# A junk row laid elsewhere, and half of the weight low parts on another engine, at the two ends of the first attention

## The chip, the cores and the metric

One core of one Trainium2 chip runs the whole program in one launch. The metric is device time in microseconds (us), given as the median of repeated runs. Five engines work side by side, each through its own list of instructions in order: TensorE (PE in the profile), VectorE (DVE), ScalarE (ACT), GpSimd (POOL) and SyncE (SP), which here only issues DMA transfers. An instruction may wait for others by semaphores. What stands behind a waiting instruction in an engine's list waits too.

## The reference

A two-layer backbone over 1024 latent tokens (`SEQ`) with 256 context tokens (`CTX_LEN`) as a prefix, 1024 wide, all in float32. The first ("even") layer's mixer is what the change touches:

```python
# even_mixer: 8 query heads and 2 key heads of 64, beside a gated linear recurrence of 4 heads of 128
oa_lat, oa_ctx = gqa_axial_attention(...)    # latent queries: softmax over all 1280 keys;
                                             # context queries: over the 256 context keys only
ob_lat, ob_ctx = hgrn2_bidirectional(...)
y_lat = concat([oa_lat, rms_norm(ob_lat) * silu(g)]) @ w_out
y_ctx = concat([oa_ctx, ...]) @ w_out
# the layer around it, for the latent tokens and with gates of their own for the context
x = x + g1 * rms_norm(y_lat, norm_post_mix)
h = rms_norm(x, norm_pre_ffn) * (1.0 + sc2) + sh2
u = conv(h @ w_up); x = x + g2 * rms_norm((silu(u_g) * u_a) @ w_down, norm_post_ffn)
```

The second ("odd") layer has a neighbourhood attention in place of this mixer, and another FFN.

## The kernel before

**Precision.** TensorE multiplies float32 values as fp32r. For more precision the kernel splits a value x into a high part `hi` (ScalarE copies x into an fp32r tile) and a low part `lo` = x - `hi` (a subtraction), and sums three products: hi hi, hi lo, lo hi. The low part of a weight of `w_out` is thus ready only after ScalarE's copy of the same weight.

**The attention.** `even_attention` goes through 40 pairs of a query block (256 queries; the context block first, then four latent blocks) and a head (8), two steps for each pair, each for 128 queries. So the first 16 steps belong to the context block, whose rows have 256 keys; the others have 1280. A step s issues, in this order: `scores` (TensorE into `g_ps` or `a_s`, and a VectorE operation that moves them to `a_p` and finds the row's minimum of the negated scores, L1103), `exponential` of the step before (ScalarE), for even s from 2 to 16 `prepare_w(s/2 - 1)`, some loads, `values` of three pairs earlier, `transposes` of two pairs earlier (TensorE into `a_pt`, L1136; ScalarE's high part `a_ph`, L1137; VectorE's low part `a_pl`, L1138) with one or two pieces of the output projection between them, `divide` of the step before (VectorE's reciprocal `rl`, L1115; GpSimd's multiplication, L1116, the "division" below) and `finish`, which on every second pair sums into `a_oT` (L1172).

**The weights of the output projection.** `prepare_w(m)`, L1056 to 1064, for m from 0 to 7: `w_out` is taken in eight tiles of 128x1024. ScalarE makes `w_hi` from `w_raw` (L1061), GpSimd subtracts into `w_lo` (L1062), and then the load of tile m + 2 is issued into the buffer of tile m, of which there are two (`w_raw`, L1056). The eight tiles fall into the context steps.

**The projection and the norms.** `project` yields one group of three matmuls at a time into `g_ps` (L136 is the line of the helper that issues each matmul), which `step` calls up. Its trailing work, the list `late`, normalizes each row block of 128 tokens: `y_half` squares a projected half on ScalarE, with the squares themselves written to a junk tile named `yjunk` and only their sum kept; VectorE scales by the gate (L364) and adds the old stream `y_x` (loaded at L1216); GpSimd stores it; `squares` squares the new stream on ScalarE, again into a junk tile (`sq_junk`, L1191); `rstd` raises to the power -1/2 on GpSimd (L144); ScalarE scales by it (L1229), and GpSimd stores the normalized rows to `xnd` in DRAM (L1230).

**The FFN behind it.** `ffn_up` begins with loads of `xnd` into tiles `n_x` (L1611), one of 128 tokens each, in the order 8, 9 (the context), 0, 1, 2, 3, then two loads of `w_up` into `w_raw` (L1530), then `n_x` 4 to 7. TensorE transposes them (`n_pv`, `n_pt`, L1344), ScalarE scales and shifts into `n_t` (L1345). The weights are split in pieces, the first of them `w_A11h` (L1546), and the first product goes into `u_g`.

**What sets the order.** The instructions of the attention on all four compute engines and on SyncE are tied to the order in which the code issues them, and so are SyncE's loads at the start of the FFN. The waits of an instruction are set by what it reads and by who last used the memory that it writes. Memory is given out by pools. Tiles of one pool (the attention's is `sp`, named "at") are laid out one behind the other in the order of their first allocation; when a stage ends, its pools' memory goes to the tiles of the next stage. So the tile that the FFN lays over a tile of the attention waits for the last user of that tile. Near the end of the attention's set-up three small tiles are allocated: `zeros` (one column of it is used, the rest is padding in multiples of `LINE`, 32 floats), `pv_t` and `sq_junk`. `sq_junk` lies under the first `n_x` tile of the FFN.

Of the kernel before, what the change touches and what calls it, by code (L numbers as in the profile page):

```python
# [11 lines left out]
F32 = mybir.dt.float32  # L12
F32R = mybir.dt.float32r
BF16 = mybir.dt.bfloat16
AF = mybir.ActivationFunctionType
OP = mybir.AluOpType
# [4 lines left out]
P = 128  # L21
# [18 lines left out]
LINE = 32  # L40
# [25 lines left out]
class Trunk:  # L66
# [958 lines left out]
    def even_attention(self, gp, tp, pp, sp):  # L1025
# [5 lines left out]
        nc, a = self.nc, self.a  # L1031
# [20 lines left out]
        def load_w(m):  # L1052
            if m < 8:
                raws[m] = self.wp.tile([P, 1024], F32, name="w_raw", bufs=2)
                k = 2 * (m % 4)
                nc.sync.dma_start(raws[m].rearrange("p (a b) -> p a b", a=2), w_out[:, k:k + 2, 512 * (m // 4):512 * (m // 4) + 512])  # L1056

        def prepare_w(m):
            raw = raws.pop(m)
            hi, lo = (self.wp.tile([P, 1024], F32R, name="w_" + x, bufs=8) for x in ("hi", "lo"))  # L1060
            nc.scalar.copy(hi, raw)  # L1061
            nc.gpsimd.tensor_tensor(out=lo, in0=raw, in1=hi.bitcast(F32), op=OP.subtract)  # L1062
            W[m] = hi, lo
            load_w(m + 2)

# [121 lines left out]
                st["ready"] = b  # L1187

        def squares(y, ms):
            for h in range(2):  # L1190
                nc.scalar.activation(yjunk, y[:, 512 * h:512 * h + 512], AF.Square, scale=1.0 / 32.0, accum_out=ms[:, h:h + 1])  # L1191

        late = []

# [49 lines left out]
                elif late:  # L1244
                    late.pop(0)()

        zeros = sp.tile([P, 2 * LINE], F32, name="zeros", bufs=1)[:, 0:1]
        nc.vector.memset(zeros, 0.0)
        pv_t = sp.tile([P, QB], F32, name="pv_t", bufs=1)
        yjunk = sp.tile([P, 512], BF16, name="sq_junk", bufs=1)  # L1250
        N = 2 * len(pairs)
        later = {4: lambda: load_keys(0, 0), 6: lambda: load_keys(0, 1), 8: lambda: load_values(0, NT - 2),
                 10: lambda: load_keys(1, 0), 12: lambda: load_keys(1, 1), 14: lambda: load_gate(1)}
# [1 line left out]
        with self.in_order(*self.compute, E.SP):  # L1255
# [8 lines left out]
            for s in range(N + 8):  # L1264
                pair, half = s // 2, s % 2
                if s < N:
                    if half == 0 and pair:
                        load_q(pair + 2)
                    scores(s)
                if 0 <= s - 1 < N:  # L1270
                    exponential(s - 1)
                if 2 <= s < 18 and half == 0:
                    prepare_w(s // 2 - 1)
                later.pop(s, lambda: None)()
                if 0 <= pair - 3 < len(pairs):
                    values(pair - 3, half)
                t = transposes(pair - 2, half) if 0 <= pair - 2 < len(pairs) else iter(())
                next(t, None)
                step(1)
                next(t, None)  # L1280
                step(1)
                next(t, None)
                if 0 <= s - 1 < N:
                    divide(s - 1)
                if 0 <= pair - 3 < len(pairs) and half == 1:
                    finish(pair - 3)
                for _ in range(min(len(todo), 1 + len(todo) // 3)):
                    todo.pop(0)()
# [1579 lines left out]
```

## Time and profile before

| | us |
|---|---|
| median of 3 runs (lowest, highest) | 3322.68 (3320.38, 3323.68) |
| the profiled execution | 3321.63 |
| its span in the trace | 3319.9 |
| mean granted TensorE clock | 0.972 |

The profile is of one execution, whose own time is 1.05 us below the median. The span is what the trace covers; 1.73 us lie around it. The page's first part gives each engine's busy time, its share of the span and its number of instructions. A group's row gives the line, the engine, the operation, output<-input with shapes, the count (x8), then the busy sum in us and the mean of one in ns, and the idle time just before them with what ended it. A row of waits names the waiting engine with its tile and line, then the engine, tile and line that it waited for, then the sum, the count and the longest. A row of the timeline gives start, duration, engine, line, operation, output<-input; a bracket tells how long the engine was idle before and who ended that. "SPq" is the queue of SyncE. The row of a stretch gives each engine's busy time and count, then the granted clock, the mean share of the DMA engines, and GB/s.

### The profile page before, as it was taken

What the parts mean: (1) busy time and instruction counts of PE and PEld (TensorE: products, weight loads), DVE (VectorE), ACT (ScalarE), POOL (GpSimd) and SP (SyncE); (2) the same over time, 40 slices, a digit from 0 to 9 for tenths busy, and PEclk for the clock granted to TensorE, in tenths of its full rate; (3) what the DMA queues carried; (4) which work ended last, traced back from release to release, by engine and by line L of the source; (5) the groups of instructions that cost most, each with busy time, mean ns of one, the idle gap of its engine ahead of it and who ended that gap; (6) DMA issues with size and microseconds to landing.
All of it is one profiled execution on the core that took longest, in us unless ns stands there. A gap on an engine that the chain in (4) does not pass through costs nothing.

```text
span 3319.9 us, 48782 instructions
## 1 busy us (share of the span) xinstructions
PE 3097.1 (93%) x18364; PEld 2547.6 (77%) x18364; DVE 2019.6 (61%) x3386; ACT 1502.2 (45%) x2681; POOL 1562.5 (47%) x1181
## 2 busy tenths in 40 slices
PE   7989999789997899999999989999998989999997
PEld 4766777478886688888878768898986768888785
DVE  4366666567774654554577862477775555555778
ACT  3232232366664543343344442566665434434443
POOL 1130111487773566666510111677764367777202
PEclk8999999889998899999999989999998989999998
DMA  6534311721114121211385772222224212222856
GB/s 249 197 103 133 119 49 38 271 73 60 48 61 153 41 76 69 75 67 66 108 288 195 264 229 107 73 63 61 63 81 155 90 64 88 84 77 89 281 179 218
DMA packets 203357, 398.73 MB, mean 120 GB/s; under 512 B 23521, under 2 KB 85473, under 8 KB 203121
## 3 DMA queue, kind: packets, MB, share of 16 engines
q1 hardware_dynamic: 192512, 358.89, 32.1%
q0 software_dynamic: 10608, 36.72, 2.9%
q8 instruction: 144, 2.36, 0.3%
q14 instruction: 93, 0.75, 0.1%
HBM read 316.86 MB, written 79.06 MB: 119 GB/s over the span
## 4 chain that ended last, share of the span: by engine, by line
PE 72%; DVE 11%; ACT 3%; DMA 3%; issue 3%; POOL 2%; SPq 0%; POOLq 0%; DVEq 0%; ACTq 0%
PE g_ps L136 18%; PE u_g L136 14%; PE d_ps L136 11%; PE u_v L136 10%; PE u_pc L136 4%; PE a_pv L136 2%; PE c_pv L136 2%; PE c_s L136 2%; PE c_pt L2503 2%; PE a_pt L1136 2%; DVE a_pl L1138 1%; PE o_ps L136 1%; PE a_s L136 1%; ACT a_ph L1137 1%; DMA d_rawB<-in_w_down 1%
## 5 line engine op out<-in xcount | busy, mean ns | idle before, releaser
L144 POOL TENSOR_TENSOR rs_r<-rs_e,mhalf 128x1 f32<-128x1 f32 (+3 forms) x106 | 85.7, 809 | 855.7 <-DVE rs_e L143 805.7
L136 PE MATMUL d_ps<-d_Bl,d_Ah 128*128 128x512 f32 x704 | 276.7, 393 | 4.1 <-DVE d_Bl L1874 3.5
L136 PE MATMUL d_ps<-d_Bh,d_Ah 128*128 128x512 f32 x704 | 275.5, 391 | 2.8 <-ACT d_Ah L1873 1.8
L136 PE MATMUL d_ps<-d_Bh,d_Al 128*128 128x512 f32 x704 | 275.7, 392 | 2.0 <-DVE d_Al L1874 1.9
L2486 POOL TENSOR_SCALAR c_p<-c_p,rl 128x640 f32<-128x640 f32 (+1 forms) x128 | 232.5, 1818 | 95.4 <-DVE rl L2485 61.8
L1116 POOL TENSOR_SCALAR a_p<-a_p,rl 128x1280 f32<-128x1280 f32 (+1 forms) x80 | 240.3, 3007 | 55.8 <-DVE rl L1115 49.5
L136 PE MATMUL g_ps<-xh,w_hi 128*128 128x512 f32 (+1 forms) x640 | 256.7, 401 | 5.6 <-DVE hq L748 3.5
L136 PE MATMUL g_ps<-xh,w_lo 128*128 128x512 f32 (+1 forms) x640 | 237.5, 371 | 1.3 <-POOL w_lo L2386 1.3
L136 PE MATMUL g_ps<-xl,w_hi 128*128 128x512 f32 (+1 forms) x640 | 237.7, 371 | 0.0
L1138 DVE TENSOR_TENSOR a_pl<-a_pt,a_ph 128x512 fp32r<-128x512 f32 (+1 forms) x200 | 119.0, 602 | 95.6 <-ACT a_ph L1137 95.5
L1561 DVE TENSOR_TENSOR f_u<-u_v,f_p 128x512 f32<-128x512 f32 x88 | 60.5, 688 | 183.7 <-PE u_v L136 183.7
L1547 POOL TENSOR_TENSOR w_S4l<-w_s,w_S4h 128x512 fp32r<-128x512 f32 x44 | 57.2, 1299 | 229.7 <-ACT w_S4h L1546 229.7
L136 PEld LDWEIGHTS d_ps<-d_Bl,d_Ah 128*128 128x128 f32 x704 | 132.7, 188 | 36.7 <-DVE d_Bl L1874 8.6
L136 PEld LDWEIGHTS d_ps<-d_Bh,d_Ah 128*128 128x128 f32 x704 | 132.8, 189 | 32.6 <-ACT d_Ah L1873 3.1
L136 PEld LDWEIGHTS d_ps<-d_Bh,d_Al 128*128 128x128 f32 x704 | 132.9, 189 | 30.0 <-DVE d_Al L1874 3.3
L1137 ACT CAST a_ph<-a_pt 128x512 fp32r<-128x512 f32 (+1 forms) x200 | 102.0, 518 | 108.6 <-PE a_pt L1136 108.5
L2506 DVE TENSOR_TENSOR c_pl<-c_pt,c_ph 128x256 fp32r<-128x256 f32 (+1 forms) x256 | 112.9, 470 | 57.9 <-ACT c_ph L2505 56.8
L136 PE MATMUL g_ps<-w_hi,xh 128*128 128x512 f32 (+1 forms) x368 | 143.2, 389 | 4.7 <-DVE xh L2260 2.1
L136 PEld LDWEIGHTS g_ps<-xh,w_hi 128*128 128x128 f32 x640 | 121.4, 190 | 31.0 <-issue 14.3
L136 PE MATMUL g_ps<-w_lo,xh 128*128 128x512 f32 (+1 forms) x368 | 137.6, 374 | 4.1 <-DVE w_lo L2247 2.9
L2505 ACT CAST c_ph<-c_pt 128x256 fp32r<-128x256 f32 (+1 forms) x256 | 98.4, 414 | 91.6 <-PE c_pt L2503 89.5
L136 PEld LDWEIGHTS g_ps<-xh,w_lo 128*128 128x128 f32 x640 | 121.0, 189 | 24.1 <-POOL w_lo L2386 1.7
(570 smaller groups left out, 9902.6 us busy)
## 6 DMA issues: line engine op xcount, KB each, us to landing
m_raw<-in_w_mod SPq DMA_DIRECT2D x96, 512.0 KB
w_raw<-in_w_up SPq DMA_DIRECT2D x88, 512.0 KB
d_rawA<-actd SPq DMA_DIRECT2D x77, 512.0 KB
d_rawB<-in_w_down SPq DMA_DIRECT2D x74, 512.0 KB
actd<-f_t SPq DMA_DIRECT2D x22, 640.0 KB
d_t<-in_w_down SPq DMA_DIRECT2D x22, 512.0 KB
actd<-f_t SPq DMA_DIRECT2D x22, 512.0 KB
d_s<-actd SPq DMA_DIRECT2D x20, 512.0 KB
```

The lines of the kernel that those rows point to most:

```text
L136: return self.nc.tensor.matmul(out, lhsT, rhs, start=start, stop=stop, skip_group_check=True, **k)
L144: nc.gpsimd.tensor_tensor(out=r[:p, :n], in0=e[:p, :n], in1=self.mhalf[:p, :n], op=OP.pow)
L1116: nc.gpsimd.tensor_scalar(Pt[:, :nk], Pt[:, :nk], rl, None, op0=OP.mult)
L1136: nc.tensor.transpose(pt[:, m, qt * P:(qt + 1) * P], Pt[:, kts[j + m] * P:(kts[j + m] + 1) * P], self.ident)
L1137: nc.scalar.copy(ph[:, j:j + n], pt[:, :n])
L1138: nc.vector.tensor_tensor(out=pl[:, j:j + n], in0=pt[:, :n], in1=ph[:, j:j + n].bitcast(F32), op=OP.subtract)
L1547: nc.gpsimd.tensor_tensor(out=lo, in0=part(j, name), in1=hi.bitcast(F32), op=OP.subtract)
L1561: nc.vector.tensor_tensor(out=out, in0=x, in1=y, op=OP.add)
L2486: nc.gpsimd.tensor_scalar(Pt[:, :n], Pt[:, :n], rl, None, op0=OP.mult)
L2503: nc.tensor.transpose(pt[:, j, :], Pt[:, (src + j) * P:(src + j + 1) * P], self.ident)
L2505: nc.scalar.copy(vap(ph, o, dims), pt[:, :cnt])
L2506: nc.vector.tensor_tensor(out=vap(pl, o, dims), in0=pt[:, :cnt], in1=vap(ph, o, dims).bitcast(F32), op=OP.subtract)
```

## The change

Two edits, both in `even_attention`. In `prepare_w` the low part of every odd tile (m = 1, 3, 5, 7) is subtracted by VectorE, that of the even ones by GpSimd as before. `squares` no longer writes to the tile `sq_junk`, which is gone; it allocates the junk tile under the name that `y_half` uses, `yjunk`, of which there is one buffer, so both write to the same place, where `y_half`'s junk is laid. And `zeros` is padded to 6 x 32 floats instead of 2 x 32, so that the tiles allocated behind it begin 512 bytes further on, `pv_t` among them; as `sq_junk` took 1024 bytes, those behind that begin 512 bytes earlier.

```diff
@@ prepare_w @@
             nc.scalar.copy(hi, raw)
-            nc.gpsimd.tensor_tensor(out=lo, in0=raw, in1=hi.bitcast(F32), op=OP.subtract)
+            eng = nc.vector if m % 2 else nc.gpsimd
+            eng.tensor_tensor(out=lo, in0=raw, in1=hi.bitcast(F32), op=OP.subtract)
             W[m] = hi, lo
@@ squares @@
         def squares(y, ms):
+            junk = sp.tile([P, 512], BF16, name="yjunk", bufs=1)
             for h in range(2):
-                nc.scalar.activation(yjunk, y[:, 512 * h:512 * h + 512], AF.Square, scale=1.0 / 32.0, accum_out=ms[:, h:h + 1])
+                nc.scalar.activation(junk, y[:, 512 * h:512 * h + 512], AF.Square, scale=1.0 / 32.0, accum_out=ms[:, h:h + 1])
@@ set-up @@
-        zeros = sp.tile([P, 2 * LINE], F32, name="zeros", bufs=1)[:, 0:1]
+        zeros = sp.tile([P, 6 * LINE], F32, name="zeros", bufs=1)[:, 0:1]
         nc.vector.memset(zeros, 0.0)
         pv_t = sp.tile([P, QB], F32, name="pv_t", bufs=1)
-        yjunk = sp.tile([P, 512], BF16, name="sq_junk", bufs=1)
```

TensorE's list is the same as before. Lines from 1062 on are one higher in the changed kernel, those behind `squares` two (up to the removed allocation), and one again in the FFN.

SyncE at the end of the attention: the last three loads of the old stream (`y_x`) and the first of the FFN's input (`n_x`). A bracket names the semaphores that a load waits for: DMAHW and DMASW for transfers, Activation for ScalarE, DVE for VectorE, Pool for GpSimd. Before:

```order
L1216 DMA y_x<-in_x 128x1024 [waits DMAHW6_49,DMASW5_49,Activation_49]
L1216 DMA y_x<-in_x 128x1024 [waits DMAHW7_49,DMASW7_49,Activation_49]
L1611 DMA n_x<-xnd 128x1024 [waits DMAHW0_49,DVE_49,Activation_49]
L1611 DMA n_x<-xnd 128x1024 [waits DMAHW1_49,PE_49]
L1611 DMA n_x<-xnd 128x1024 [waits DMAHW2_49,Pool_49]
```

And now:

```order
L1218 DMA y_x<-in_x 128x1024 [waits DMAHW6_49,DMASW5_49,Activation_49]
L1218 DMA y_x<-in_x 128x1024 [waits DMAHW7_49,DMASW7_49,Activation_49]
L1612 DMA n_x<-xnd 128x1024 [waits DMAHW0_49,DVE_49]
L1612 DMA n_x<-xnd 128x1024 [waits DMAHW1_49,PE_49]
L1612 DMA n_x<-xnd 128x1024 [waits DMAHW2_49,Pool_49]
```

The order of the loads is the same. The first `n_x` load no longer waits for ScalarE (the last user of `sq_junk`), only for VectorE, whose last sum into `a_oT` lies in the same memory.

VectorE in the context steps, around the low part of weight tile 1 (a_p and nm are the scores and their row minimum, a_pl the low part of the transposed probabilities, rl the reciprocal of the row's sum). Before:

```order
L1103 ISA a_p,nm<-g_ps,zeros 128x256 [waits PE_49]
L1103 ISA nm 128x1
L1138 TENSOR_TENSOR a_pl_6617<-a_pt,a_ph_6616 128x512 [waits Activation_49]
L1115 RECIPROCAL rl<-l 128x1
L1103 ISA a_p,nm<-g_ps,zeros 128x256 [waits PE_49]
```

And now:

```order
L1104 ISA a_p,nm<-g_ps,zeros 128x256 [waits PE_49]
L1104 ISA nm 128x1
L1063 TENSOR_TENSOR w_lo<-w_raw,w_hi 128x1024 [waits DMAHW6_49,DMAHW4_49,DMAHW7_49,DMAHW3_49,Activation_49]
L1139 TENSOR_TENSOR a_pl_6616<-a_pt,a_ph_6615 128x512 [waits Activation_49]
L1116 RECIPROCAL rl<-l 128x1
L1104 ISA a_p,nm<-g_ps,zeros 128x256 [waits PE_49]
```

The low part stands between the row minimum and `a_pl` of the same step, and waits for ScalarE's `w_hi` and for transfers.

GpSimd in the same steps, with the divisions (`a_p<-a_p,rl`) of the context block and the low parts of the weights. Before:

```order
L1116 TENSOR_SCALAR a_p<-a_p,rl 128x256 [waits DVE_49] x2
L1062 TENSOR_TENSOR w_lo<-w_raw,w_hi 128x1024 [waits DMAHW3_49,DMAHW2_49,DMAHW6_49,DMAHW0_49,DMAHW7_49,PE_49,Activation_49]
L1116 TENSOR_SCALAR a_p<-a_p,rl 128x256 [waits DVE_49] x2
L1062 TENSOR_TENSOR w_lo<-w_raw,w_hi 128x1024 [waits DMAHW1_49,DMAHW2_49,DMAHW0_49,Activation_49]
L1116 TENSOR_SCALAR a_p<-a_p,rl 128x256 [waits DVE_49]
```

And now:

```order
L1117 TENSOR_SCALAR a_p<-a_p,rl 128x256 [waits DVE_49] x2
L1117 TENSOR_SCALAR a_p<-a_p,rl 128x256 [waits DVE_49,Activation_49]
L1117 TENSOR_SCALAR a_p<-a_p,rl 128x256 [waits DVE_49]
L1063 TENSOR_TENSOR w_lo<-w_raw,w_hi 128x1024 [waits DMAHW2_49,DMAHW1_49,DMAHW3_49,DMAHW0_49,DMAHW6_49,PE_49,Activation_49]
L1117 TENSOR_SCALAR a_p<-a_p,rl 128x256 [waits DVE_49]
```

Of four divisions in a row none has a low part between them any more; the low part of the next even tile comes behind the fourth.

## The prediction

> **What bounds the kernel now.** The page's first part gives busy time over the whole span; the windows give it for single stretches, here the context phase of the first attention (643.2 to 676.3), the end of its projection, and three stretches from there into the FFN.
>
> ```profile
> PE 3097.1 (93%) x18364; PEld 2547.6 (77%) x18364; DVE 2019.6 (61%) x3386; ACT 1502.2 (45%) x2681; POOL 1562.5 (47%) x1181
> ...
> core 0: us, PE busy (x) PEld busy (x) DVE busy (x) ACT busy (x) POOL busy (x), PEclk, DMA share, GB/s
> 643.20:676.30 33.10, 22.24 (x88) 16.74 (x86) 14.05 (x53) 22.09 (x50) 32.71 (x24) 0.63 0.81 272
> 1020.00:1052.80 32.80, 31.39 (x149) 25.91 (x149) 12.40 (x24) 14.33 (x34) 9.68 (x16) 1.00 0.31 120
> 1052.80:1063.20 10.40, 0.00 (x0) 0.03 (x1) 3.73 (x7) 3.28 (x7) 2.24 (x4) 0.70 0.44 158
> 1063.20:1073.20 10.00, 6.37 (x20) 3.17 (x20) 4.04 (x12) 3.32 (x7) 0.00 (x0) 0.50 1.02 368
> 1073.20:1078.40 5.20, 3.92 (x21) 3.62 (x21) 4.02 (x6) 5.17 (x9) 2.54 (x2) 0.59 1.03 414
> ```
>
> TensorE is the bound overall (93%), but in neither place that the change touches. In the context phase it is GpSimd, busy 32.71 of 33.10 us. Between attention and FFN TensorE does nothing for 10.4 us, and after that the DMA engines are full (1.02) while they were at 0.44 and 0.31 before. Something holds the loads back. SyncE's own waits name it, and the timeline places it:
>
> ```profile
> SPq L1611 <- ACT sq_junk L1191: 15.8, 1, 15.8
> ...
> 1027.34 0.42 DVE L1172 TENSOR_TENSOR a_oT<-a_pv,pv_t 64x256 f32<-64x256 f32 x1 [3.17 <-ACT pv_t L1170]
> 1043.18 0.33 SPq L1216 DMA_DIRECT2D y_x<-in_x  x1
> 1052.38 0.39 PE L136 MATMUL g_ps<-w_hi,a_ol 128*128 128x512 f32 x1
> 1058.39 0.19 ACT L1191 ACTIVATION_READ_ACCUMULATOR sq_junk<-y 128x1 f32 x1
> 1058.61 0.63 ACT L1191 ACTIVATE sq_junk<-y 128x512 bf16<-128x512 f32 x1
> 1059.36 3.03 SPq L1611 DMA_DIRECT2D n_x<-xnd  x6
> 1060.45 1.15 ACT L1229 ACTIVATE y_x<-y,rs_r 128x1024 f32<-128x1024 f32 x1 [1.12 <-POOL rs_r L144]
> 1061.89 0.57 POOL L1230 DMA_DIRECT2D xnd<-y_x  x1 [1.48 <-ACT y_x L1229]
> 1062.49 1.05 SPq L1530 DMA_DIRECT2D w_raw<-in_w_up  x2
> 1063.20 0.45 PE L1344 MATMUL n_pv<-ident,n_x 128*128 128x128 f32 x1 [10.44 <-DMA n_x<-xnd]
> 1065.23 0.56 ACT L1345 ACTIVATE n_t<-n_pv,mod,mod 128x256 f32<-128x256 f32 x1 [3.63 <-PE n_pv L1344]
> 1068.83 0.56 ACT L1345 ACTIVATE n_t<-n_pt,mod,mod 128x256 f32<-128x256 f32 x1
> 1073.16 0.62 ACT L1546 CAST w_A11h<-w_raw 128x512 fp32r<-128x512 f32 x1 [3.77 <-DMA w_raw<-in_w_up]
> 1078.35 0.47 PE L136 MATMUL u_g<-x_B110h,w_A11h 128*128 128x512 f32 x1
> ```
>
> The first FFN input load waits 15.8 us for the last square of the attention. Six input loads and two of w_up then go out together from 1059.36, and ScalarE's first weight split waits for w_up until 1073.16. The chain of waits runs through just that:
>
> ```profile
> 1062.49 10.65 DMA w_raw<-in_w_up
> ```
>
> **The junk row.** By the change's order the first n_x load waits for a DVE operation alone; this is the last sum into a_oT, over at 1027.76. The load is then held only by SyncE's order: the last y_x load ahead of it goes out at 1043.18 and takes 0.33. The six n_x loads can go from about 1043.5, 15.8 us earlier. They are 512 KB each (128x1024 f32), 3.15 MB; at the 368 GB/s of the full stretch they are in by 1052.1. The DMA engines were at 0.31 there, so there is room. Next in the queue, the w_up load still waits for TensorE's last projection product (row at 1052.38, over at 1052.77). It goes then; both are 1.05 MB, 2.9 us at that rate, in by about 1057.
>
> What is late next? ScalarE works in order, and its last attention operation, L1229, ends at 1060.45 + 1.15 = 1061.60. Nothing in the change moves that. So the first n_t goes from 1065.23 to about 1061.65. Six of them took from 1065.23 to 1069.39 (1068.83 + 0.56), 4.16 us: over at 1065.81 now. The weight split behind them, at 1073.16 before, finds its data since 1057 and starts at about 1065.85: 7.3 us earlier. The stretch from there to the first u_g product (1078.35 - 1073.16 = 5.2 us) holds DVE and ScalarE work that doesn't change. **First term: -7.3 us.** Bounds: if w_up or the later tiles come late again, only the first n_t's gain is left, -3.6; if everything followed SyncE it would be -15.8, but ScalarE's 1061.60 excludes more than 1073.16 - 1061.65 = -11.5. I take -7.3, as every step of it has a row. The new waits of squares and y_half on each other's junk are waits of ScalarE for its own earlier work; the pair of squares has such a wait already (0.03 us between 1058.39 + 0.19 and 1058.61), so the nine rows that gain one cost between 0 and 0.3 us, and I take 0. All other tiles of this pool move by 512 bytes, which I cost at nothing.
>
> **The low parts.** Four of eight subtractions leave GpSimd for VectorE:
>
> ```profile
> L1062 POOL TENSOR_TENSOR w_lo<-w_raw,w_hi 128x1024 fp32r<-128x1024 f32 x8 | 19.0, 2376 | 1.6 <-ACT w_hi L1061 1.6
> L539 DVE TENSOR_TENSOR w_lo<-w_raw,w_hi 128x1024 fp32r<-128x1024 f32 x10 | 12.1, 1222 | 4.1 <-ACT w_hi L538 4.1
> ...
> PE a_pt L1136 <- POOL a_p L1116: 7.0, 5, 2.8
> SPq L1056 <- POOL w_lo L1062: 17.9, 6, 3.5
> ...
> 653.76 1.83 POOL L1116 TENSOR_SCALAR a_p<-a_p,rl 128x256 f32<-128x256 f32 x2
> 653.85 1.03 ACT L1061 CAST w_hi<-w_raw 128x1024 fp32r<-128x1024 f32 x1
> 654.75 0.55 PE L1136 MATMUL a_pt<-ident,a_p 128*128 128x128 f32 x3 [0.56 <-POOL a_p L1116]
> 655.39 0.59 ACT L1137 CAST a_ph<-a_pt 128x512 fp32r<-128x512 f32 x1 [0.51 <-PE a_pt L1136]
> 655.56 2.38 POOL L1062 TENSOR_TENSOR w_lo<-w_raw,w_hi 128x1024 fp32r<-128x1024 f32 x1
> 656.01 0.69 DVE L1138 TENSOR_TENSOR a_pl<-a_pt,a_ph 128x512 fp32r<-128x512 f32 x1 [1.72 <-ACT a_ph L1137]
> 656.62 0.15 DVE L1115 RECIPROCAL rl<-l 128x1 f32<-128x1 f32 x1
> 657.89 1.85 POOL L1116 TENSOR_SCALAR a_p<-a_p,rl 128x256 f32<-128x256 f32 x2
> ```
>
> GpSimd gives up 4 x 2.376 = 9.5 us, VectorE takes on 4 x 1.222 = 4.9. The 9.5 are no gain in time, since a second loop is close behind. One pair of heads takes 657.89 - 653.76 = 4.13 us: two divisions, one low part. Without the low part the next division waits for the chain division, transposes, a_ph, a_pl, reciprocal, which is over at 656.77: about 3.1 us after 653.76. An odd pair thus gains 1.04 at most, four of them 4.2. On VectorE the new row stands ahead of a_pl and waits for w_hi; w_hi ends at 654.88, a_pl starts at 656.01, so of its 1.22 us all but 0.1 are hidden. If VectorE must share with GpSimd it is longer:
>
> ```profile
> 803.71 0.73 POOL L1162 TENSOR_TENSOR a_ol<-a_oT,a_oh 128x256 fp32r<-128x256 f32 x1
> 803.74 1.79 DVE L364 SCALAR_TENSOR_TENSOR y<-y,rs_r,gate 128x1024 f32<-128x1024 f32 x1
> 1055.28 1.29 DVE L364 SCALAR_TENSOR_TENSOR y<-y,rs_r,gate 128x1024 f32<-128x1024 f32 x1 [0.75 <-POOL rs_r L144]
> ```
>
> Beside a GpSimd operation the same VectorE operation with two tile inputs took 1.79 instead of 1.29. The divisions of 653.76 run just when the new row wants to start (654.88), so I add that 0.5: a gain of 0.5 per odd pair, **second term -2.2 us**. Its bounds: -4.2 without sharing, and 0 if the loads set the pace (DMA share 0.81 over the phase, though low parts that end sooner also release w_raw sooner, a wait of 17.9 us in SyncE's row); below nothing it costs time if a new row holds back its pair by more than 1.04, taken up as a rival.
>
> The Trainium skill, page Trainium Architecture — The Big Picture, section What this means for kernel authors, says that VectorE and GpSimd contend for a shared pair of SBUF ports, and that this is an exclusive lock and not a split of bandwidth. By that rule the new row would wait until both divisions are over (655.59) and end at 656.81, 0.8 past the start of a_pl; an odd pair would gain 0.24, the four -1.0, and the time would be 3314.4. The row of 1.79 agrees with the rule as far as it goes, since 0.5 is less than the 0.73 of the GpSimd operation beside it; no row here shows it for a division.
>
> **Sum.** -7.3 - 2.2 = -9.5 us. Both places lie one behind the other, and what follows starts from them, so both shifts carry to the end. The profiled execution took 3321.63 us (span 3319.9) and would take 3312.1; the median of the runs, 3322.68, is 1.05 above it, so I forecast 3313.2.
>
> **Rivals.**
> *A, the transition gives only its first part.* The later tiles (n_x 4 to 7, the last one stored after 1061.9) or w_up land late and hold ScalarE again. For it: the stretch 1063.2 to 1073.2 is all DMA. Against it: the six early loads are then no longer in the way. -3.6 - 2.2 = -5.8: 3316.9, within 0.2%. Chance 0.14.
> *B, more than forecast.* VectorE shares for free and w_hi no longer waits for w_raw: -7.3 - 4.2 = -11.5, some more if the lower idle time raises the granted clock (0.63 in the phase): 3311 or less. Chance 0.12.
> *C, slower: GpSimd holds VectorE up.* VectorE, with a_pl, reciprocal and row minimum queued behind its low part, waits for the low part of the next pair and both divisions, 2.38 + 1.85 + 1.22 = 5.45 us in each odd pair: 4 x 5.45 - 9.5 = +12.3, with the first term +5.0: 3327.7. It turns the sum positive from 4.2 us per odd pair ((7.3 + 9.5) / 4). Against it: beside GpSimd the quoted row grew by 0.5, not by four, and w_hi is over before the next pair's low part can start. Chance 0.05.
> *D, the change doesn't do what it says.* The n_x load finds another late owner of its space. The only wait shown is a_oT at 1027.76, so 0.02, at 3320.5.
>
> **How the numbers follow.** The forecast (-6.6 to -11) has 0.67. About 0.2% (6.6 us) is what a measurement of this kernel can tell from no change. Faster by more: the forecast and B, 0.67 + 0.12, less 0.03 for its lower edge: 0.76. Within: A, D and that edge, 0.19. Slower by more than 0.2% takes C in full: 0.05. The range runs from 3308 (both upper bounds, -11.5 and -4.2, would be 3307) to 3319 (A with no second term, 3319.1).
>
> **What would show it.** The SyncE wait on the squares' junk is gone and the first n_x load goes out within 1 us of the last y_x load; TensorE's transposes start before ScalarE's L1229 ends; w_A11h starts within 1 us of the sixth n_t, and the stretch from the last projection product to the first u_g product falls from 25.6 to about 18.3 us. In the context phase GpSimd's busy time falls by 9.5 and shows gaps, and the phase is 2 us shorter. Wrong it is if w_A11h waits for w_raw again, or if the new VectorE rows take over 2.3 us.

## The result and the profile after

The changed kernel takes 3315.04 us (median of 20 runs, 3308.21 to 3322.15) against 3324.73 us for the kernel before (20 runs beside them, 3317.06 to 3329.13). The ratio is 0.9972, 95% interval 0.9966 to 0.9979: about 9.3 us faster (7.0 to 11.3). Forecast were 9.5. One execution each in two of the experiments below (3976.76 us with the w_up loads ahead on the kernel before, 10145.22 us with the divisions on VectorE and all low parts on GpSimd) ran far longer than all others, and the ratios leave them out.

The profiled execution took 3316.76 us, its span is 3315.0. That is only 4.9 us below the profiled execution of before, which is no measure of the change: single executions differ by some microseconds ahead of the attention, where both kernels run the same instructions. The first division of the attention stands at 640.99 before and at 650.29 now. So stretches are compared here, not places in the span.

The transition, from SyncE's waits and the timeline of the kernel after (start, duration, engine, line, operation):

```profile
SPq L1612 <- DMA xnd<-y_x: 11.4, 2, 7.8
SPq L1531 <- PE g_ps L136: 6.1, 1, 6.1
...
1049.33 0.33 SPq L1218 DMA_DIRECT2D y_x<-in_x  x1
1049.75 2.90 SPq L1612 DMA_DIRECT2D n_x<-xnd  x6
1058.46 0.39 PE L136 MATMUL g_ps<-w_hi,a_ol 128*128 128x512 f32 x1
1058.88 0.85 SPq L1531 DMA_DIRECT2D w_raw<-in_w_up  x2
1060.41 0.44 PE L1345 MATMUL n_pv<-ident,n_x 128*128 128x128 f32 x2 [1.56 <-DVE y L355]
1066.59 1.15 ACT L1231 ACTIVATE y_x<-y,rs_r 128x1024 f32<-128x1024 f32 x1 [1.12 <-POOL rs_r L144]
1067.65 0.55 ACT L1346 ACTIVATE n_t<-n_pv,mod,mod 128x256 f32<-128x256 f32 x1
1071.69 0.61 ACT L1547 CAST w_A11h<-w_raw 128x512 fp32r<-128x512 f32 x1
1076.91 0.48 PE L136 MATMUL u_g<-x_B110h,w_A11h 128*128 128x512 f32 x1
```

The wait for the squares' junk, 15.8 us, is gone; what is left are waits for stores of `xnd` and for the last projection product. The six loads go out 0.42 us after the last `y_x` load, those of w_up right behind the last projection product. TensorE transposes at 1060.41, 7.2 us before ScalarE takes the first result at 1067.65, and from there to `w_A11h` none of ScalarE's rows waits for a load or a transpose any more. From the last projection product to the first u_g product it is 1076.91 - 1058.46 = 18.45 us, and was 1078.35 - 1052.38 = 25.97: 7.52 less.

The context block, before (first fence) and after, from GpSimd's and VectorE's timeline with the first latent scores (`a_s`) at its end; GpSimd's rows of "x2" are the two divisions of a pair:

```profile
640.99 0.92 POOL L1116 TENSOR_SCALAR a_p<-a_p,rl 128x256 f32<-128x256 f32 x1
670.37 1.62 PE L136 MATMUL a_s<-K,a_q 128*128 128x512 f32 x3 [1.20 <-DMA a_q<-q2d]
```

```profile
650.29 0.92 POOL L1117 TENSOR_SCALAR a_p<-a_p,rl 128x256 f32<-128x256 f32 x1
654.83 2.37 POOL L1117 TENSOR_SCALAR a_p<-a_p,rl 128x256 f32<-128x256 f32 x2
655.18 1.22 DVE L1063 TENSOR_TENSOR w_lo<-w_raw,w_hi 128x1024 fp32r<-128x1024 f32 x1 [1.73 <-ACT w_hi L1061]
658.29 1.82 POOL L1117 TENSOR_SCALAR a_p<-a_p,rl 128x256 f32<-128x256 f32 x2 [1.09 <-DVE rl L1116]
662.45 1.83 POOL L1117 TENSOR_SCALAR a_p<-a_p,rl 128x256 f32<-128x256 f32 x2
663.57 1.34 DVE L1063 TENSOR_TENSOR w_lo<-w_raw,w_hi 128x1024 fp32r<-128x1024 f32 x1 [0.62 <-ACT w_hi L1061]
670.96 2.86 POOL L1117 TENSOR_SCALAR a_p<-a_p,rl 128x256 f32<-128x256 f32 x2
671.88 1.24 DVE L1063 TENSOR_TENSOR w_lo<-w_raw,w_hi 128x1024 fp32r<-128x1024 f32 x1 [0.61 <-ACT w_hi L1061]
678.02 1.19 PE L136 MATMUL a_s<-K,a_q 128*128 128x512 f32 x2 [0.98 <-DMA a_q<-q2d]
```

The first odd pair now takes 658.29 - 654.83 = 3.46 us, the even one behind it 662.45 - 658.29 = 4.16 (both were 4.13), and GpSimd waits 1.09 for VectorE's reciprocal, for which it never waited in this block before. The next two odd pairs take 3.55 and 3.54 (were 4.13). The fourth takes 4.37 (was 4.20): its low part (682.05) stands behind VectorE's first row minimum of 1280 keys, and it gains nothing. From the first division to the first latent scores it is 27.73 us, and was 29.38: 1.65 less. Two of the three pairs of divisions that meet a low part on VectorE take 2.37 and 2.86 us instead of 1.82; the third, at 662.45, takes 1.83.

### The profile page after: what moved, and what is told of

Same layout as the page of the kernel before. It is cut to its first block, busy times and chain, and to the rows that moved or that the text cites. A ratio compares the mean times of both kernels' runs of the same rounds, so it can differ in the third digit from the quotient of the medians.

```text
span 3315.0 us, 48787 instructions
## 1 busy us (share of the span) xinstructions
PE 3102.2 (94%) x18364; PEld 2553.2 (77%) x18364; DVE 2024.0 (61%) x3390; ACT 1501.5 (45%) x2681; POOL 1553.1 (47%) x1177
## 4 chain that ended last, share of the span: by engine, by line
PE 73%; DVE 11%; ACT 3%; issue 3%; DMA 2%; POOL 1%; SPq 0%; DVEq 0%; POOLq 0%; ACTq 0%
PE g_ps L136 18%; PE u_g L136 14%; PE d_ps L136 11%; PE u_v L136 10%; PE u_pc L136 4%; PE a_pv L136 2%; PE c_pv L136 2%; PE c_s L136 2%; PE c_pt L2504 2%; PE a_pt L1137 2%; DVE a_pl L1139 1%; PE a_s L136 1%; PE o_ps L136 1%; ACT a_ph L1138 1%; DVE d_Bl L1875 1%
```

## The experiments

Times without a ratio are of single runs. A ratio is to the kernel before, run beside it; it is worked out over the executions of a comparison, and it differs from the quotient of the two medians by up to 0.0005. The stretch "transition" is from the start of the last projection product to that of the first u_g product, "context" from the first division to the first latent scores.

### The junk row alone

The kernel before with the edits in `squares` and the set-up, `prepare_w` as it was.

> The junk row and the padding alone; all low parts stay on GpSimd. Theory: the whole first term is in the transition. The first n_x load goes out within 1 us of the last y_x load; from the last projection product to the first u_g product 18.5 us instead of 26.0; the context phase stays as before (pairs of 4.13 us); ratio to before 0.9977 (-7.5 us). Rival (the gain of the two edits together is not a sum, the transition gives only the first n_t): 22 us in that stretch, ratio 0.9989. Rival (the two traces differ by chance): ratio 0.9995 or more.

Measured: 3316.29 us, ratio 0.9978 (0.9968 to 0.9988). From its timeline, both ends of the transition and of the context:

```profile
643.29 0.92 POOL L1116 TENSOR_SCALAR a_p<-a_p,rl 128x256 f32<-128x256 f32 x1
672.62 2.05 PE L136 MATMUL a_s<-K,a_q 128*128 128x512 f32 x4 [0.92 <-DMA a_q<-q2d]
...
1052.19 0.39 PE L136 MATMUL g_ps<-w_hi,a_ol 128*128 128x512 f32 x1
1070.65 0.47 PE L136 MATMUL u_g<-x_B110h,w_A11h 128*128 128x512 f32 x1
```

Transition 18.46, context 29.33 (before 29.38). The first term is all of this edit, and it stands in the transition alone.

### The low parts alone

The kernel before with the edit in `prepare_w` only.

> The low parts of the odd tiles on VectorE alone; the junk row stays where it was. Theory: the odd pairs of the context block take 3.5 us instead of 4.13, the even ones stay, and the context phase is 2.5 to 3.4 us shorter: ratio 0.9991; the wait of n_x for sq_junk stays at 15 to 16 us. Rival (VectorE and GpSimd exclude each other): divisions beside a VectorE low part are longer by its 1.2 us, the phase is 1 us shorter, ratio 0.9997. Rival (the loads of w_raw set the pace): 0, ratio 1.0000.

Measured: 3323.14 us, ratio 0.9994 (0.9985 to 1.0002). SyncE's wait, and the ends of the context:

```profile
SPq L1612 <- ACT sq_junk L1192: 15.8, 1, 15.8
...
644.37 0.92 POOL L1117 TENSOR_SCALAR a_p<-a_p,rl 128x256 f32<-128x256 f32 x1
671.98 2.05 PE L136 MATMUL a_s<-K,a_q 128*128 128x512 f32 x4 [0.64 <-DMA a_q<-q2d]
```

Context 27.61, 1.8 less than before: more than the rival's 1, less than the theory's 2.5 to 3.4, as only three of the four odd pairs are shorter (3.47, 3.55 and 3.54; the fourth takes 4.52). The time alone does not tell this from nothing, since its interval holds 1.0000; the stretch does, and it repeats the 1.65 of the full change. In the three traces with all low parts and divisions on GpSimd and the padding as in the kernel before or the changed one, the context is 29.33 to 29.54, in the four with the odd low parts alone on VectorE 27.61 to 28.46. The two ratios multiply to 0.9972, that of the full change: as far as intervals about 0.002 wide can tell, the terms add up.

### All eight low parts on VectorE

```diff
-            eng = nc.vector if m % 2 else nc.gpsimd
+            eng = nc.vector
```

> The changed kernel with all eight low parts on VectorE. Theory (a pair without a low part on GpSimd takes 3.5 us): the even pairs fall from 4.2 to 5.0 us to 3.5 too, 3 to 5 us more; ratio to before 0.9960. Rival (a low part on VectorE holds up GpSimd's divisions for as long as it runs): the even pairs stay over 4 us, ratio as the changed kernel, 0.9972. Rival (VectorE's low part holds back a_pl): some pairs over 4.5 us and a ratio above 0.9972.

Measured: 3313.39 us, ratio 0.9968 (0.9957 to 0.9980). The pairs on GpSimd's timeline, with VectorE's rows in one of them:

```profile
655.72 1.83 POOL L1117 TENSOR_SCALAR a_p<-a_p,rl 128x256 f32<-128x256 f32 x2 [2.00 <-DVE rl L1116]
657.48 1.23 DVE L1063 TENSOR_TENSOR w_lo<-w_raw,w_hi 128x1024 fp32r<-128x1024 f32 x1 [1.20 <-ACT w_hi L1061]
657.69 0.59 ACT L1138 CAST a_ph<-a_pt 128x512 fp32r<-128x512 f32 x1 [0.24 <-PE a_pt L1137]
658.62 0.68 DVE L1139 TENSOR_TENSOR a_pl<-a_pt,a_ph 128x512 fp32r<-128x512 f32 x1
659.54 1.83 POOL L1117 TENSOR_SCALAR a_p<-a_p,rl 128x256 f32<-128x256 f32 x2 [2.00 <-DVE rl L1116]
```

The first three pairs, odd or even, take 3.82 to 3.86 us (659.54 - 655.72 = 3.82): longer than 3.46, shorter than 4.16. The theory's 3.5 us, and its 3 to 5 us more, did not come. Here the low part falls behind the divisions and stretches none; but `a_ph` is over at 658.28 and `a_pl` starts only when the low part ends, 0.34 later. That is the mechanism of the last rival, but small. From 648.15 to 675.22 the context is 27.07, 0.7 less than in the changed kernel, too little for the times to tell.

### The w_up loads ahead of the input loads

```diff
                 for i, t in tags.items():
-                    if i == 4:
+                    if i == 8:
                         load(0, 0)
                         load(0, 1)
```

Made twice, on the kernel before and on the changed one. A third load of w_up moves ahead with them.

> The kernel before (junk row as before, n_x held until the last square) with the w_up loads issued ahead of the n_x loads. It takes apart the two halves of the first term. Theory: the first n_t stays where it was, but w_A11h follows the sixth n_t at once, 3.7 us earlier: ratio 0.9989, and from the last projection product to the first u_g product 22.3 us instead of 26.0. Rival (the six input loads are pushed back by the 1.5 MB ahead of them, or the end is set by n_x alone): 26 us in that stretch, ratio 1.0000.

> The changed kernel with the w_up loads issued ahead of the n_x loads, so that the six input loads again wait, now for the last projection product instead of the last square. It asks whether the early n_x loads or w_up's place carry the first term. Theory (both loads out of the way of ScalarE): six input loads then share the DMA engines with 1.5 MB of w_up and come too late for ScalarE's 9.2 us, and the stretch from the last projection product to the first u_g product is 20 to 23 us instead of 18.5. Rival (only w_up's place counts): 18.5 us.

Measured on the kernel before: 3321.60 us, ratio 0.9993 (0.9983 to 1.0002); on the changed one, a single run of 3317.54. The timelines, first on the kernel before, then on the changed one:

```profile
1054.12 0.39 PE L136 MATMUL g_ps<-w_hi,a_ol 128*128 128x512 f32 x1
1067.95 0.56 ACT L1345 ACTIVATE n_t<-n_pv,mod,mod 128x256 f32<-128x256 f32 x1 [4.62 <-PE n_pv L1344]
1072.02 0.61 ACT L1546 CAST w_A11h<-w_raw 128x512 fp32r<-128x512 f32 x1
1078.19 0.78 PE L136 MATMUL u_g<-x_B110h,w_A11h 128*128 128x512 f32 x1
```

```profile
1057.42 0.39 PE L136 MATMUL g_ps<-w_hi,a_ol 128*128 128x512 f32 x1
1065.75 0.45 PE L1345 MATMUL n_pv<-ident,n_x 128*128 128x128 f32 x1 [7.95 <-DMA n_x<-xnd]
1079.26 0.49 PE L136 MATMUL u_g<-x_B110h,w_A11h 128*128 128x512 f32 x1
```

On the kernel before `w_A11h` follows the sixth n_t without a wait, 17.90 us after the last projection product instead of 20.78, so this half of the term is there; but the first n_t is 1.0 later than before (13.83 after the product, was 12.85), with 1.5 MB of weights ahead of the input in the queue, another 1.0 goes behind `w_A11h` (6.17 us to the first u_g product, was 5.19), and the transition is 24.07, not 22.3. On the changed kernel the same order costs: 21.84 instead of 18.45, within the theory's 20 to 23. TensorE waits for the input again (7.95), yet the first n_t is only 0.84 later than in the changed kernel; most of the loss, 2.5 us, falls behind `w_A11h` (1071.51, so 7.75 us to the first u_g product instead of 5.22), where TensorE waits 1.00 and 1.04 us for later input loads. So w_up's early place alone is worth 1.9 of the 7.5 us. Early input loads with w_up as late as before were not run.

### The divisions on VectorE

```diff
-            nc.gpsimd.tensor_scalar(Pt[:, :nk], Pt[:, :nk], rl, None, op0=OP.mult)
+            (nc.vector if nk == CTX else nc.gpsimd).tensor_scalar(Pt[:, :nk], Pt[:, :nk], rl, None, op0=OP.mult)
```

On the changed kernel, once with all low parts on GpSimd and once with the odd ones on VectorE.

> The changed kernel, with the divisions of the context block (256 keys) on VectorE and all eight low parts back on GpSimd. Theory: GpSimd's three operations in one pair set the pace, so with two of them gone GpSimd has 2.4 us per pair and a pair falls from 4.13 (odd 3.5 in the changed kernel) to about 3.0 us, set by ScalarE's five operations (2.7 us); from the first division to the first latent scores 25 us instead of 27.7; ratio to before 0.9963. Rival (the odd pairs already run at what the loads of w_raw allow): pairs of 3.5 us, as the changed kernel's odd ones; ratio 0.9970. Rival (the two engines exclude each other, and VectorE with divisions waits for GpSimd's low parts): pairs of 4 us or more, ratio 0.9977.

> The changed kernel as it is (odd low parts on VectorE), with the divisions of the context block on VectorE too. Theory: VectorE has 1.2 us more in every second pair, and GpSimd nothing there; pairs about 3.0 us, ratio 0.9963, within 0.0005 of the version with all low parts on GpSimd. Rival (mutual exclusion costs the version with low parts on GpSimd): this one is faster than that by 3 us or more.

Measured: 3320.55 us, ratio 0.9994 (0.9985 to 1.0004), and 3316.98 us, ratio 0.9984 (0.9975 to 0.9993): both above the changed kernel's 0.9972, though the second's interval meets that one's at the edge. The second is 3.6 us faster than the first by their medians, as its rival had it (3 or more), with intervals that overlap too. From the first's timeline, the divisions of one pair (the last two) and the last one of the pair ahead, of which the middle one meets a low part on GpSimd; from the second's, the same place in two pairs that follow each other, the second of them with no GpSimd low part or division, and ScalarE's exponential ahead of it:

```profile
666.16 0.35 DVE L1117 TENSOR_SCALAR a_p<-a_p,rl 128x256 f32<-128x256 f32 x1
668.91 2.36 POOL L1063 TENSOR_TENSOR w_lo<-w_raw,w_hi 128x1024 fp32r<-128x1024 f32 x1 [0.71 <-ACT w_hi L1061]
669.48 0.69 DVE L1139 TENSOR_TENSOR a_pl<-a_pt,a_ph 128x512 fp32r<-128x512 f32 x1 [2.06 <-ACT a_ph L1138]
670.28 1.15 DVE L1117 TENSOR_SCALAR a_p<-a_p,rl 128x256 f32<-128x256 f32 x1
671.88 0.35 DVE L1117 TENSOR_SCALAR a_p<-a_p,rl 128x256 f32<-128x256 f32 x1
```

```profile
657.37 0.51 ACT L1111 ACTIVATE a_p<-a_p,nm 128x256 f32<-128x256 f32 x1 [1.59 <-DVE nm L1104]
657.45 0.35 DVE L1117 TENSOR_SCALAR a_p<-a_p,rl 128x256 f32<-128x256 f32 x1
662.09 0.35 DVE L1117 TENSOR_SCALAR a_p<-a_p,rl 128x256 f32<-128x256 f32 x1
```

The division beside the low part takes 1.15 instead of 0.35 and ends at 671.43, 0.16 after GpSimd's low part (671.27). So do the other seven in this trace that stand beside one: they take 1.02 to 1.85 and end 0.14 to 0.16 us after it. `a_pl`, which reads one of its inputs from PSUM (`a_pt`), is at its usual 0.69. The theory of 3.0 us per pair fell: the pair of the first fence takes 671.88 - 666.16 = 5.72 us (the others 4.50 to 5.73), that of the second 662.09 - 657.45 = 4.64, though GpSimd has neither a division nor a low part in it. The row of 1.59 belongs to the pair ahead of that: ScalarE waits there for the row minimum, which stands in VectorE's list behind a division of 1.28 beside GpSimd's low part (654.48 to 656.84). What makes 4.64 of the pair behind it was not isolated. The loss carries on into the latent scores, whose first row minimum on VectorE (128x1280) starts 34.12 and 33.92 us after the first division, and 30.35 in the changed kernel.

### The last scaling on another engine

```diff
-late.append(lambda y=y, xt=xt: nc.scalar.mul(xt, y, st["r2"]))
+late.append(lambda y=y, xt=xt, e=(b == 4 and i == 1): nc.gpsimd.tensor_scalar(xt, y, st["r2"], None, op0=OP.mult) if e else nc.scalar.mul(xt, y, st["r2"]))
```

> The changed kernel, with the last scaling of the attention (last row block only) taken from ScalarE and given to GpSimd. It asks what ends last in the transition now. Theory (ScalarE's order, as in the prediction: its last attention operation holds back the first n_t): the first n_t starts 2 us sooner after the last projection product (7.1 us instead of 9.2) and the first u_g product follows it 16.5 us after, instead of 18.5. Rival (the last rows' store, 2.4 us later by GpSimd, holds the last n_x tiles): first n_t sooner, u_g no earlier than 18.5 us or later.

Measured: 3313.79 us in a single run.

```profile
1056.31 0.39 PE L136 MATMUL g_ps<-w_hi,a_ol 128*128 128x512 f32 x1
1063.23 0.55 ACT L1346 ACTIVATE n_t<-n_pv,mod,mod 128x256 f32<-128x256 f32 x1
1064.62 2.87 POOL L1231 TENSOR_SCALAR y_x<-y,rs_r 128x1024 f32<-128x1024 f32 x1
1064.80 1.22 DVE L1334 TENSOR_TENSOR x_ctx0l<-n_t,x_ctx0h 128x256 fp32r<-128x256 f32 x1
1073.93 0.48 PE L136 MATMUL u_g<-x_B110h,w_A11h 128*128 128x512 f32 x1
```

The first n_t comes 6.92 us after the product (9.19 in the changed kernel): it was ScalarE's order that held it. But the transition is 17.62, only 0.8 less, not the theory's 16.5. VectorE's low part of the input, 0.42 or 0.43 where GpSimd is idle, takes 1.22 beside GpSimd's scaling, and the next n_t waits 0.90 for it. The scaling does not hold VectorE up all the time: the two operations behind that low part (1065.95 and 1066.26) take their usual 0.28 and 0.43, though it runs on to 1067.49.

### Both small gains together

All eight low parts on VectorE, and the last scaling on VectorE.

> The changed kernel with all eight low parts on VectorE and the last scaling of the attention (last row block) on VectorE instead of ScalarE. Theory: 0.7 us from the context block (first division to first latent scores 27.1 us), and in the transition VectorE's 0.75 us in place of ScalarE's 1.15, with no GpSimd operation to stretch VectorE's casts: first u_g product 17.8 us after the last projection product instead of 18.5; together 1.4 us, ratio to before 0.9965, not to be told from the changed kernel's 0.9972 by the time alone. Rival (gains in these stretches are given back behind them): both stretches shorter, ratio 0.9972 or above.

Measured: 3311.99 us, ratio 0.9965 (0.9953 to 0.9977). Transition 17.57, context 27.19. It is the fastest of the versions by its median, but its interval covers the changed kernel's 0.9972.

### The junk row without the padding

> The junk row alone, without the padding of zeros, so that the tiles behind lie 1024 bytes lower instead of 512. Theory (the place of these tiles costs nothing, only the wait of n_x counts): as the junk row with padding, first u_g product 18.5 us after the last projection product, ratio 0.9977. Rival (the padding does part of the work): over 19 us there, or a ratio above 0.9985.

Measured: 3316.57 us, ratio 0.9986 (0.9976 to 0.9995); transition 18.44. SyncE's wait for the first load of the attention's keys, without padding (first, with the first key product behind it) and with it:

```profile
SPq L1070 <- DVE mod L339: 12.0, 1, 12.0
...
645.44 1.20 PE L136 MATMUL g_ps<-K_0c,a_q 128*128 128x256 f32 x4 [5.30 <-DMA a_q<-q2d]
```

```profile
SPq L1070 <- DMA gate_bw<-in_gate_b: 0.4, 1, 0.4
```

My theory was wrong: the padding does part of the work. With its tile 512 bytes lower than in the changed kernel the load of the first keys, and with it all of the attention's first loads, waits 12.0 us for a VectorE operation of the stage ahead (L339, the table `mod`), and TensorE stands for 5.30 us; with the padding it waits 0.4 us for a transfer. The transition has the same gain; about 3 us are lost at the other end of the attention. The ratios say so (0.0008 of 3322) with intervals that overlap; in the traces it is 37.37 us from GpSimd's last gating operation of the stage ahead (L1020) to the first latent scores without the padding, and 34.07 with it.

## Why the prediction was right

**The junk row.** Right in every step. The prediction counted the transition from the end of the last projection product (25.6 to about 18.3); by that count it is 18.06 now. The numbers here count from its start. Loads: forecast within 1 us of the last `y_x` load, measured 0.42. Sixth n_t followed by `w_A11h` without a wait: so it is. -7.3 was forecast for the transition, -7.52 measured with both edits and -7.51 with this one alone. What was late next, ScalarE's last scaling, was named rightly: taking it away moves the first n_t by 2.3 us. Rival A (w_up or the later tiles late again) did not come.

**The low parts.** The term was -2.2; the context is 1.65 us shorter in the full change and 1.8 with this edit alone. The size is near, but that is partly luck: three of its steps were off, and they cancel in part.

- *Sharing.* The prediction added 0.5 us to VectorE's new row. That row takes 1.22 to 1.34 us, and 1.22 on a quiet engine. It is GpSimd's divisions that grow, 2.37 and 2.86 us for two instead of 1.82, and that in two of three pairs.
- *The length of a pair.* 3.1 us is not what a pair takes without GpSimd's low part: the changed kernel's shortest is 3.46, and 3.82 with none there, so an odd pair could gain 0.67 and not 1.04, and the upper bound of -4.2 could not be reached. The 3.1 (3.01 by its rows) was read from the pair at 653.76 of the kernel before, in which the granted clock was 0.95 and three transposes of TensorE took 0.55 us together. In the pair ahead of it they took 0.90 (650.60), with a clock of 0.50 from 643.20 to 653.76, and from the division's start to the reciprocal's end it was 3.35 us (649.62 to 652.97). The changed kernel ran this phase at 0.50.
- *The number of pairs.* Three gained, 0.58 to 0.67 us each, and the fourth nothing.

Rival C (VectorE held up by four microseconds) did not come, and B's free sharing was not there; the granted clock, which B hoped to see rise, was 0.50 in the stretch from 652.50 to 683.30 against 0.63 before; it was 0.52 in this phase with the junk row alone (645.60 to 678.60), so the low parts are not shown to have lowered it.

```profile
652.50:683.30 30.80, 24.15 (x85) 18.65 (x85) 18.10 (x55) 21.25 (x50) 25.10 (x20) 0.50 0.86 293
```

This stretch ends 0.84 us before the last division of the block. Counted alike, from GpSimd's first low part to the start of that division, GpSimd is down from 32.78 of 33.17 us to 25.10 of 31.64. It is no longer busy throughout, as forecast. Its busy time fell by 7.7 us and not 9.5, mainly because its divisions grew, and the phase is 1.5 us shorter, not 2.

**The rule on shared ports.** The Trainium skill's page Trainium Architecture — The Big Picture, section What this means for kernel authors, calls the contention of VectorE and GpSimd an exclusive lock. The traces bear that out in part, and there better than my 0.5 did: each of the eight divisions on VectorE that stood beside a GpSimd low part ended only 0.14 to 0.16 us after it. Other rows do not fit a lock held for a whole operation: the low part at 663.57 began while GpSimd's second division was running, and took 1.34 us beside a row of 1.83; and two VectorE operations ran at their usual length beside GpSimd's last scaling. Where I went wrong with the rule was who waits: VectorE's low part did not wait for the divisions, it held up the second one in two pairs, and the cost fell on an engine that had time left. The 3314.4 that I worked out from it assumed the opposite.

**At nothing.** The shared junk cost nothing that a row shows. The move of the other tiles by 512 bytes cost nothing either (34.14 us from GpSimd's last gating operation to the first latent scores before, 34.07 with the junk row alone), but as the last experiment shows not because such a move is harmless. The prediction gave no reason for its nothing, so that was luck.

## What to carry to other kernels

A scratch tile that nobody reads can still be the last user of an address, and a load of the next stage then waits for it: look at SyncE's longest wait, find what lies under the tile, and move the scratch to where a late user does no harm. When it is moved, look at both ends of the stage, since every tile laid out behind it moves too. In taking work off one of GpSimd and VectorE and giving it to the other, count what stands beside it at that moment, and which of the two has time to wait.

## What the runs showed that I had not expected

TensorE stops at the same place ahead of the attention in nine of the twelve profiled executions, in the middle of a row of 32 like matmuls, and waits for nothing that the profile shows ("issue"). In the changed kernel, behind the first 21 of them:

```profile
613.46 0.37 PE L136 MATMUL h_pa<-hQ,hKM 128*32 128x32 f32 x10 [3.61 <-issue]
```

It lasted 1.69 to 3.87 us where it came, and was absent in the kernel before, in the junk row alone and in the version with both small gains. TensorE's list is the same in all of them, and what decides whether it stops stays open. It makes up part of the 9.3 us by which the profiled execution of the changed kernel reached the attention later.
